# The opening of a hybrid decoder layer: memory rows turned before they are normed, and the memory keys and values projected for two row tiles per weight tile

## The chip, the cores and the metric

The kernel runs on one core of a Trainium2 chip. The metric is the device time of one execution in microseconds (us); three runs of the kernel before gave 2234.21, 2238.23 and 2239.06 us, and the median, 2238.23 us, is what the change is held against. Everything is computed in float32; matmuls run as three passes over operands that are split into a high and a low part.

## The reference

One layer, a sequence of 1024 tokens of width 1024, and 256 memory tokens. What the change touches is the norm of x and the preparation of the memory keys and values:

```python
h = rms_norm(x, norm_mix_g[l])
proj = h @ w_in[l]
...
def memory_cross_attention(q, mem, mem_g, w_kv, q_g, k_g):
    qh = rms_norm(q.reshape(bsz, seq, C_HEADS, C_DQK), q_g)
    mkv = rms_norm(mem, mem_g) @ w_kv
    mk, mv = jnp.split(mkv, [C_Q_W], axis=-1)          # 512 key columns, 1024 value columns
    mk = rms_norm(mk.reshape(bsz, -1, C_HEADS, C_DQK), k_g)
    ...
```

`rms_norm` multiplies each row by one number (the inverse root mean square of the row) and each column by a gain. Everything after (three branches, gates, output projection, MLP) is the same in both kernels.

## The kernel before, in words

`phase_x` is the opening, roughly the first 66 us of the program. It produces `hT` (the normed x, turned so that features lie on partitions, as a high and a low part for each of 8 feature blocks k), `mkT` (the turned memory keys) and `mv` (the memory values). The rest of the program needs all three; `branch_c`, which follows at once, starts with 24 matmuls for each of 8 token tiles on `hT`.

- **Memory.** Two tiles `mx` of 128 memory rows are loaded. `norm_rows` squares and sums a row on ScalarE (ACT, L231), turns the sum into 1/rms on GpSimd (POOL, L127 and L128) and multiplies the tile in place on VectorE (DVE, L233). Then TensorE (PE) transposes the tiles (L243, bank `tp`), and `split` writes the result as high part (ACT, L114) and low part (DVE, L115) into `memT`, with the gain.
- **Weights.** `load_w` brings `in_wkv` in pieces of 512 KB (`raw`, L137), and splits each into a high part (ACT, L111) and a low part (DVE, L112) in a tile `w`, which holds two of the eight blocks k. There are three buffers for `raw` and four for `w`.
- **Projections.** Group 0 of `wkv` gives the keys, groups 1 and 2 the values. For each group `proj` runs one row tile after the other: 8 blocks times three matmuls (`mm3`, L91) into one PSUM bank `mm`. A finished key tile is copied (L266), squared (L268), reduced per head (L270), turned into 1/rms (L127, L128), scaled (L273), transposed (L276) and split into `mkT`.
- **x.** Eight tiles `xk` are loaded (L293), normed the same way (L231, L127, L128, L233), transposed (L94, bank pair `sc`) and split into `hT`.

All DMAs are issued by one queue, SyncE's (SP), in order. Each engine executes its own queue in order. In `phase_x` the order of each queue is made by the framework's scheduler, which moves instructions of different steps past each other on PE as well; from `branch_c` on PE's order is pinned to the program's.

Of the kernel before, what the change touches and what calls it, by code (L numbers as in the profile page):

```python
# [10 lines left out]
F32 = mybir.dt.float32  # L11
F32R = mybir.dt.float32r
AF = mybir.ActivationFunctionType
ALU = mybir.AluOpType
AX = mybir.AxisListType
PSUM = bass.MemoryType.PSUM

P = 128
D = 1024
S = 1024  # L20
NT = 8
NK = 8
# [5 lines left out]
R_MIX, R_MEM, R_MLP, R_MN, R_CB, R_CW, R_BG = 0, 8, 16, 24, 32, 40, 72  # L28
# [43 lines left out]
class Layer:  # L72
# [152 lines left out]
        self.nlam = d[:, 37:38]  # L225


    def norm_rows(self, src, r1, scr):

        nc = self.nc  # L230
        nc.scalar.activation(scr, src, AF.Square, accum_out=r1)  # L231
        self.rsqrt_mean(r1, r1, D, 1)
        nc.vector.tensor_scalar_mul(src, src, r1)  # L233


    def mem_kv(self, pool, tmp, xs):
        nc, a = self.nc, self.a
        memT = tmp.tile([P, NK, 2, 256], F32R, tag="memT", name="memT")
        for k in range(0, NK, 2):
            ps = self.tp_tile()  # L240
            for i in range(2):
                for t in range(2):
                    nc.tensor.transpose(  # L243
                        ps[:, (i * 2 + t) * P : (i * 2 + t + 1) * P], xs[t][:, (k + i) * P : (k + i + 1) * P], self.ident
                    )
            for i in range(2):
                self.split(
                    memT[:, k + i, 0], memT[:, k + i, 1], ps[:, i * 256 : (i + 1) * 256],
                    self.vec[:, R_MEM + k + i : R_MEM + k + i + 1],
                )  # L250
        self.mkT = pool.tile([P, 4, 2, 256], F32R, name="mkT")
        self.mv = pool.tile([P, 2, 2, D], F32R, name="mv")

        def proj(w, t):
            ps = self.mm_tile()
            for k in range(NK):
                self.mm3(
                    ps, (memT[:, k, 0, t * P : (t + 1) * P], memT[:, k, 1, t * P : (t + 1) * P]), w[k], k == 0, k == NK - 1
                )
            return ps  # L260

        w = self.load_w(a["wkv"][0], 512, 2)
        for t in range(2):
            ps = proj(w, t)
            kr = tmp.tile([P, 512], F32, tag="kr", name=self.name("kr"))
            nc.scalar.copy(kr, ps)  # L266
            scr = tmp.tile([P, D], F32, tag="sq", name=self.name("scr"))
            nc.scalar.activation(scr[:, 0:512], ps, AF.Square)  # L268
            r4 = tmp.tile([P, 4], F32, tag="r4", name=self.name("r4"))
            nc.vector.tensor_reduce(r4, scr[:, 0:512].rearrange("p (h d) -> p h d", h=4), axis=AX.X, op=ALU.add)  # L270
            self.rsqrt_mean(r4, r4, 128, 4)
            for h in range(4):
                nc.vector.tensor_scalar_mul(kr[:, h * P : (h + 1) * P], kr[:, h * P : (h + 1) * P], r4[:, h : h + 1])  # L273
            pt = self.tp_tile()
            for h in range(4):
                nc.tensor.transpose(pt[:, h * P : (h + 1) * P], kr[:, h * P : (h + 1) * P], self.ident)  # L276
            p4 = pt.rearrange("p (h t) -> p h t", h=4)
            self.split(self.mkT[:, :, 0, t * P : (t + 1) * P], self.mkT[:, :, 1, t * P : (t + 1) * P], p4)
        for g in range(2):
            w = self.load_w(a["wkv"][1 + g], 512, 2)  # L280
            yield
            for t in range(2):
                ps = proj(w, t)
                s = slice(g * 512, (g + 1) * 512)
                self.split(self.mv[:, t, 0, s], self.mv[:, t, 1, s], ps)

    def phase_x(self, kv, tmp):

        nc, a = self.nc, self.a

        def load(src, tag):
            x = tmp.tile([P, D], F32, tag=tag, name=self.name(tag))
            nc.sync.dma_start(x, src)  # L293
            return x

        def norm(x):
            r = tmp.tile([P, 1], F32, tag="r1", name=self.name("r1"))
            scr = tmp.tile([P, D], F32, tag="sq", name=self.name("scr"))
            self.norm_rows(x, r, scr)

        mem = [load(a["mem"][t * P : (t + 1) * P, :], "mx") for t in range(2)]
        for x in mem:
            norm(x)
        gen = self.mem_kv(kv, tmp, mem)
        next(gen)
        xs = [load(a["x"][t * P : (t + 1) * P, :], "xk") for t in range(NT)]

        def half(hf):
            for x in xs[4 * hf : 4 * hf + 4]:
                norm(x)  # L310
            for k in range(NK):
                if k % 2 == 0:
                    sc = self.sc_tile()
                ps = sc[:, k % 2 * 512 : k % 2 * 512 + 512]
                for i in range(4):
                    self.transpose(ps[:, i * P : (i + 1) * P], xs[4 * hf + i][:, k * P : (k + 1) * P])
                s = slice(hf * 512, (hf + 1) * 512)
                self.split(self.hT[:, k, 0, s], self.hT[:, k, 1, s], ps, self.vec[:, R_MIX + k : R_MIX + k + 1])

        half(0)  # L320
        next(gen)
        half(1)
        for _ in gen:
            pass

    def store_y(self, b, kt, hf, y):
        self.nc.sync.dma_start(self.yd[b][kt, :, hf * 512 : (hf + 1) * 512], y)
# [1426 lines left out]
```

## Time and profile before

The profiled execution has a span of 2237.1 us from its first instruction to its last, 1.1 us under the median of the runs.

| what | measured |
|---|---|
| PE busy over the span | 2180.2 us (97%) |
| DVE, ACT, POOL busy | 1394.6, 1012.0, 534.1 us |
| first transposes of memory (PE) | 12.35 us |
| first projection matmul (PE) | 14.68 us |
| last transposes of x on PE | 65.30 us |
| first transposes of `branch_c` (tile `cqr`) | 70.78 us |

Almost the whole span is PE work in a fixed order, so what the opening takes longer or shorter moves all that follows. A timeline row reads: start, duration, engine, line, operation, out<-in, count, and in brackets how long the engine sat idle before it and what ended that.

### The profile page before, as it was taken

The page shows a single profiled execution, that of the slowest core. Times are in us where ns is not written, and L with a number is a line of the kernel's source. Part 1 is how long each engine was busy: PE and PEld are TensorE (multiplying, and loading weights), DVE is VectorE, ACT ScalarE, POOL GpSimd, SP SyncE. Part 2 cuts the span into 40 slices and gives each one's busy share as a digit, 9 for nine tenths or more (in the row PEclk, how much of TensorE's full clock was granted, in tenths as well). Part 3 has the DMA queues.
Part 4 walks back from the last instruction along what each step waited for, and adds up shares of the span by engine and source line. Part 5 has one row for each costly group of instructions (what it writes and reads, how often), then busy time and mean ns, then how long its engine had stood idle before and what let it go on. Part 6 is the DMA issues. An engine that isn't in the chain of part 4 may idle for free.

```text
span 2237.1 us, 30556 instructions
## 1 busy us (share of the span) xinstructions
PE 2180.2 (97%) x11222; PEld 1875.4 (84%) x11222; DVE 1394.6 (62%) x2627; ACT 1012.0 (45%) x1994; POOL 534.1 (24%) x696
## 2 busy tenths in 40 slices
PE   7999999999999999999999999999999999899999
PEld 5778788988799999999888888887887888788887
DVE  6645456554238888888752233453588887866679
ACT  6533445443336666666643111223444444543332
POOL 2100000000001111111000002202566666565553
PEclk9999999999999999999999999999999999999999
DMA  6013222210421001110134343435525444864444
GB/s 247 20 72 114 70 65 80 67 44 29 144 69 31 26 29 39 39 36 29 54 122 141 114 139 129 151 107 182 182 99 193 155 151 155 296 202 147 147 151 168
DMA packets 113780, 247.89 MB, mean 111 GB/s; under 512 B 11065, under 2 KB 19550, under 8 KB 111582
## 3 DMA queue, kind: packets, MB, share of 16 engines
q1 hardware_dynamic: 111326, 233.36, 31.6%
q10 hardware_dynamic: 2304, 12.58, 1.4%
q8 instruction: 88, 1.44, 0.3%
q14 instruction: 62, 0.51, 0.1%
HBM read 178.76 MB, written 67.14 MB: 110 GB/s over the span
## 4 chain that ended last, share of the span: by engine, by line
PE 78%; DVE 8%; DMA 5%; ACT 4%; issue 2%; POOL 1%; SPq 0%; DVEq 0%; ACTq 0%; POOLq 0%
PE mm L91 46%; PE p L91 21%; PE sc L91 6%; PE tp L94 2%; PE po L91 2%; PE pr L94 1%; DVE w L112 1%; DVE acc L67 1%; DMA raw<-in_wd 1%; DVE u L67 1%; DVE wo L67 1%; DMA kraw<-y 1%; ACT dpe L997 1%; ACT w L111 0%; DVE c L67 0%
## 5 line engine op out<-in xcount | busy, mean ns | idle before, releaser
L91 PE MATMUL mm<-w,hT 128*128 128x384 f32 (+3 forms) x2496 | 480.7, 332 | 2.6 <-ACT w L111 1.7
L91 PE MATMUL mm<-hT,w 128*128 128x512 f32 x1920 | 464.7, 396 | 2.8 <-ACT w L111 2.6
L91 PEld LDWEIGHTS mm<-hT,w 128*128 128x128 f32 x1920 | 355.2, 189 | 76.2 <-ACT w L111 2.8
L91 PEld LDWEIGHTS mm<-w,hT 128*128 128x128 f32 x2496 | 385.8, 189 | 14.9 <-ACT w L111 2.4
L91 PE MATMUL p<-xd,wo 128*128 128x512 f32 x1344 | 309.4, 392 | 5.6 <-DVE c L67 2.2
L91 PE MATMUL p<-xo,wo 128*128 128x512 f32 x1344 | 308.2, 390 | 5.5 <-DVE st L1407 1.8
L91 PEld LDWEIGHTS p<-xd,wo 128*128 128x128 f32 x1344 | 253.4, 189 | 61.5 <-DVE c L67 3.3
L91 PEld LDWEIGHTS p<-xo,wo 128*128 128x128 f32 x1344 | 251.0, 188 | 61.3 <-DVE u L67 3.7
L91 PE MATMUL mm<-kt,w 128*128 128x512 f32 x1152 | 261.6, 389 | 0.2 <-DVE w L112 0.2
L112 DVE TENSOR_TENSOR w<-raw,w 128x256 fp32r<-128x256 f32 (+3 forms) x304 | 171.9, 589 | 141.0 <-ACT w L111 139.7
L91 PEld LDWEIGHTS mm<-kt,w 128*128 128x128 f32 x1152 | 216.1, 188 | 45.5 <-DVE w L112 0.7
L111 ACT CAST w<-raw 128x256 fp32r<-128x256 f32 (+3 forms) x304 | 154.7, 531 | 177.4 <-PE mm L91 131.6
L104 ACT CAST wo<-wraw 128x896 fp32r<-128x896 f32 x122 | 115.0, 944 | 207.6 <-PE p L91 111.5
L67 DVE TENSOR_TENSOR wo<-wraw,wo 128x896 fp32r<-128x896 f32 x122 | 145.3, 1208 | 58.2 <-ACT wo L104 58.1
L1134 POOL TENSOR_TENSOR wraw<-wraw 128x128 f32<-128x128 f32 x128 | 96.8, 757 | 239.6 <-DMA wraw<-in_wdown 118.5
L997 ACT ACTIVATE dpe<-sc,dst,drr 128x256 f32<-128x256 f32 (+7 forms) x128 | 106.7, 834 | 52.3 <-DVE dst L993 49.0
L989 DVE CUSTOM_DVE_ANT_0 sc<-sc,tmask 128x256 f32<-128x256 f32 (+7 forms) x128 | 97.1, 759 | 22.0 <-PE sc L91 22.0
L127 POOL TENSOR_SCALAR hss<-hss 128x4 f32<-128x4 f32 x8 | 3.3, 412 | 392.5 <-ACT mscr L747 272.7
L127 POOL TENSOR_SCALAR drr<-drr 128x16 f32<-128x16 f32 x16 | 3.6, 225 | 373.6 <-DVE drr L943 357.0
L1137 POOL TENSOR_TENSOR wraw<-wraw 128x128 f32<-128x128 f32 x128 | 88.5, 692 | 10.0
L1136 POOL TENSOR_TENSOR wraw<-wraw 128x128 f32<-128x128 f32 x128 | 90.7, 709 | 0.0
L104 ACT CAST xd<-xd 128x1536 fp32r<-128x1536 f32 (+2 forms) x36 | 54.9, 1528 | 69.8 <-DMA xd<-r_d 69.7
(281 smaller groups left out, 3101.0 us busy)
## 6 DMA issues: line engine op xcount, KB each, us to landing
wraw<-in_wup SPq DMA_DIRECT2D x64, 256.0 KB, 3.2
r_d<-xts SPq DMA_DIRECT2D x16, 1024.0 KB, 4.1
wraw<-in_wdown SPq DMA_DIRECT2D x64, 256.0 KB, 3.1
xd<-r_d SPq DMA_DIRECT2D x19, 768.0 KB, 7.5
xd<-r_d SPq DMA_DIRECT2D x14, 1024.0 KB, 6.6
raw<-in_wgate SPq DMA_DIRECT2D x48, 256.0 KB, 3.1
gates<-gt SPq DMA_DIRECT2D x48, 256.0 KB, 2.0
raw<-in_wd SPq DMA_DIRECT2D x32, 384.0 KB, 3.6
```

The lines of the kernel that those rows point to most:

```text
L67: return self.tc.keep_in_program_order(f(*a, **k))
L91: self.pin(self.nc.tensor.matmul(out, l, r, start=start, stop=stop))
L94: self.pin(self.nc.tensor.transpose(out, x, self.ident))
L104: self.A.copy(hi, src)
L111: nc.scalar.copy(hi, src)
L112: nc.vector.tensor_sub(lo, src, f32(hi))
L127: g.tensor_scalar(r, ss, 1.0 / width, EPS, op0=ALU.mult, op1=ALU.add)
L989: V.tensor_tensor_reduce(out=sc[:, 0:n], in0=sc[:, 0:n], in1=self.tmask[:, D - n : D], scale=1.0, scalar=-3.0e38, op0=ALU.add, op1=ALU.max ...
L997: nc.scalar.activation(pe[c][:, 0:n], sc[:, 0:n], AF.Exp, bias=t8[:, 2 + c : 3 + c], scale=rr[:, i, c : c + 1], accum_out=t8[:, 4 + c : 5 ...
L1134: G.tensor_add(r[:, 4], r[:, 0], r[:, 3])
L1136: G.tensor_sub(r[:, 6], r[:, 1], r[:, 0])
L1137: G.tensor_sub(r[:, 7], r[:, 2], r[:, 5])
```

## The change

Memory rows are transposed raw. Their 1/rms (`rm`) is applied later, as the scale of the instructions that read the projections out of PSUM: for keys the copy and the square on ACT, for values the two halves of `split`. Each weight block now serves both row tiles before the next one (6 matmuls in place of 3), with two accumulation banks open. PE's order is pinned to the program's in the whole of `phase_x`. x's tiles are normed inside the first two passes, every second one by POOL in place of DVE; the transposes of x's first half stand in the second pass (in the `tp` banks), those of its second half in the third. The numbers of matmuls (144) and transposes (88) stay the same.

```diff
+    def row_scale(self, src, r1, scr):
+        self.nc.scalar.activation(scr, src, AF.Square, accum_out=r1)
         self.rsqrt_mean(r1, r1, D, 1)
-        nc.vector.tensor_scalar_mul(src, src, r1)
...
+        self.pinned = True
+        mem = [load(a["mem"][t * P : (t + 1) * P, :], "mx") for t in range(2)]
+        rm = [scale(x, f"rm{t}") for t, x in enumerate(mem)]
...
+        def proj(w, ps, k):
+            for t in range(2):
+                c = slice(t * P, (t + 1) * P)
+                self.mm3(ps[t], (memT[:, k, 0, c], memT[:, k, 1, c]), w[k], k == 0, k == NK - 1)
+
+        def keys(t, ps):
+            kr = tmp.tile([P, 512], F32, tag=f"kr{t}", name=self.name("kr"))
+            nc.scalar.activation(kr, ps, AF.Copy, scale=rm[t])
             scr = tmp.tile([P, D], F32, tag="sq", name=self.name("scr"))
+            nc.scalar.activation(scr[:, 0:512], ps, AF.Square, scale=rm[t])
...
+        def norm(t):
+            r = scale(xs[t])
+            (nc.gpsimd if t % 2 else nc.vector).tensor_scalar_mul(xs[t], xs[t], r)
+
+        w = self.load_w(a["wkv"][0], 512, 2)
+        mem_turn(0)
+        mem_turn(2)
+        xs.extend(load(a["x"][t * P : (t + 1) * P, :], "xk") for t in range(NT))
+        ps = [self.mm_tile() for _ in range(2)]
+        for k in range(NK):
+            proj(w, ps, k)
+            if k in (1, 3):
+                mem_turn(k + 3)
+            if k >= 4:
+                norm(k - 4)
+        kr = [keys(t, ps[t]) for t in range(2)]
+        w = self.load_w(a["wkv"][1], 512, 2)
+        sv = self.sc_tile()
+        pv = [sv[:, 0:512], sv[:, 512:]]
+        for k in range(NK):
+            proj(w, pv, k)
+            if k < 4:
+                norm(4 + k)
+            else:
+                x_turn(0, 2 * k - 8)
+                x_turn(0, 2 * k - 7)
+        values(0, pv)
+        w = self.load_w(a["wkv"][2], 512, 2)
+        ps = [self.mm_tile() for _ in range(2)]
+        for k in range(NK):
+            if k in (1, 3):
+                key_turn(k // 2, kr[k // 2])
+            proj(w, ps, k)
+            x_turn(1, k)
+        values(1, ps)
+        self.pinned = False
```

One stretch shows how the queues read now: the passage from the key pass to the first value pass, on ACT and on DVE. PE has nothing between the last key matmul and the first matmul on the values' first weight piece in the change; before, the second key tile's matmuls followed the first key tile's. In these rows the first number of a name is its running number: `xk_18` to `xk_25` are x's eight tiles in the change; `raw_8`, `raw_10`, `raw_12`, `raw_14` and `w_9` to `w_15` belong to the key pass; `w_45` to `w_51` to the first value pass; `kr_38` and `kr_41` are the two key tiles.

ACT in the change, from the square of the fourth x tile to the second weight piece of the first value pass:

```order
L230 ACTIVATE scr_37_294,r1_36_293<-xk_21_197 128x1024
L274 ACTIVATE kr_38_299<-mm_26_207,r1_4_140 128x512
L276 ACTIVATE scr_39_301<-mm_26_207,r1_4_140 128x512
L274 ACTIVATE kr_41_311<-mm_27_208,r1_6_145 128x512
L276 ACTIVATE scr_42_313<-mm_27_208,r1_6_145 128x512
L230 ACTIVATE scr_54_351,r1_53_350<-xk_22_199 128x1024
L230 ACTIVATE scr_56_363,r1_55_362<-xk_23_201 128x1024
L230 ACTIVATE scr_58_375,r1_57_374<-xk_24_203 128x1024
L111 CAST w_45_325<-raw_44_323 128x1024
L230 ACTIVATE scr_60_387,r1_59_386<-xk_25_205 128x1024
L111 CAST w_47_330<-raw_46_328 128x1024
```

And in the kernel before, from the last weight piece of the keys (`w_19`) on:

```order
L111 CAST w_19_208<-raw_18_206 128x1024
L114 ACTIVATE memT_152<-tp_11_180,vec_76 128x256
L111 CAST w_31_301<-raw_30_299 128x1024
L266 COPY kr_21_236<-mm_20_211 128x512
L268 ACTIVATE scr_22_238<-mm_20_211 128x512
L111 CAST w_33_306<-raw_32_304 128x1024
L111 CAST w_35_311<-raw_34_309 128x1024
```

The first weight piece of the values (`w_31` before, `w_45` now) stood ahead of the first key tile's copy; now it stands behind both key tiles' copies and squares and three squares of x.

DVE in the kernel before, over the same stretch:

```order
L112 TENSOR_TENSOR w_19_208<-raw_18_206,w_19_208 128x1024
L115 SCALAR_TENSOR_TENSOR memT_152<-tp_11_180,vec_76,memT_152 128x256
L112 TENSOR_TENSOR w_31_301<-raw_30_299,w_31_301 128x1024
L270 TENSOR_REDUCE r4_23_240<-scr_22_238 128x4
L273 TENSOR_SCALAR kr_21_236<-kr_21_236,r4_23_240 128x128 x4
L112 TENSOR_TENSOR w_33_306<-raw_32_304,w_33_306 128x1024
```

There the low part of the values' first weight piece (`w_31`) came ahead of the first key tile's norm. DVE in the change, from the first key tile's norm on (`r4_40` and `r4_43` are the key tiles' statistics, `r1_53` and `r1_57` those of `xk_22` and `xk_24`):

```order
L278 TENSOR_REDUCE r4_40_303<-scr_39_301 128x4
L281 TENSOR_SCALAR kr_38_299<-kr_38_299,r4_40_303 128x128 x4
L278 TENSOR_REDUCE r4_43_315<-scr_42_313 128x4
L312 TENSOR_SCALAR xk_22_199<-xk_22_199,r1_53_350 128x1024
L281 TENSOR_SCALAR kr_41_311<-kr_41_311,r4_43_315 128x128 x4
L312 TENSOR_SCALAR xk_24_203<-xk_24_203,r1_57_374 128x1024
L112 TENSOR_TENSOR w_45_325<-raw_44_323,w_45_325 128x1024
L112 TENSOR_TENSOR w_47_330<-raw_46_328,w_47_330 128x1024
```

The low part of `w_45` now stands behind the norms of both key tiles and the scaling of `xk_22` and `xk_24`. The statistics `r1` of x have two buffers, so the square of `xk_24` (which writes `r1_57`) waits until `xk_22` has been scaled with `r1_53`.

More of the change, by code (lines that the diff above doesn't have):

```diff
@@ L225, in consts @@
         self.nlam = d[:, 37:38]
-    def norm_rows(self, src, r1, scr):
-        nc = self.nc
-        nc.scalar.activation(scr, src, AF.Square, accum_out=r1)
+    def row_scale(self, src, r1, scr):
+        self.nc.scalar.activation(scr, src, AF.Square, accum_out=r1)
         self.rsqrt_mean(r1, r1, D, 1)
[L233 to L285, printed above, removed]
@@ L294, in load, with scale @@
             return x
-        def norm(x):
-            r = tmp.tile([P, 1], F32, tag="r1", name=self.name("r1"))
+        def scale(x, tag="r1"):
+            r = tmp.tile([P, 1], F32, tag=tag, name=self.name("r1"))
             scr = tmp.tile([P, D], F32, tag="sq", name=self.name("scr"))
-            self.norm_rows(x, r, scr)
+            self.row_scale(x, r, scr)
+            return r
+        self.pinned = True
         mem = [load(a["mem"][t * P : (t + 1) * P, :], "mx") for t in range(2)]
-        for x in mem:
-            norm(x)
@@ L304, in phase_x @@
[L304 to L311, printed above, removed]
-                if k % 2 == 0:
[L313 to L324, printed above, removed]
+        rm = [scale(x, f"rm{t}") for t, x in enumerate(mem)]
+        memT = tmp.tile([P, NK, 2, 256], F32R, tag="memT", name="memT")
+        self.mkT = kv.tile([P, 4, 2, 256], F32R, name="mkT")
+        self.mv = kv.tile([P, 2, 2, D], F32R, name="mv")
+        def mem_turn(k):
+            ps = self.tp_tile()
+            for t in range(2):
+                for i in range(2):
+                    j = i * 2 + t
+                    self.transpose(ps[:, j * P : (j + 1) * P], mem[t][:, (k + i) * P : (k + i + 1) * P])
+            for i in range(2):
+                self.split(
+                    memT[:, k + i, 0], memT[:, k + i, 1], ps[:, i * 256 : (i + 1) * 256],
+                    self.vec[:, R_MEM + k + i : R_MEM + k + i + 1],
+                )
@@ new lines, in proj @@
+        def proj(w, ps, k):
+            for t in range(2):
+                c = slice(t * P, (t + 1) * P)
[3 more added lines that the diff above has]
+            nc.scalar.activation(kr, ps, AF.Copy, scale=rm[t])
+            scr = tmp.tile([P, D], F32, tag="sq", name=self.name("scr"))
+            nc.scalar.activation(scr[:, 0:512], ps, AF.Square, scale=rm[t])
+            r4 = tmp.tile([P, 4], F32, tag="r4", name=self.name("r4"))
+            nc.vector.tensor_reduce(r4, scr[:, 0:512].rearrange("p (h d) -> p h d", h=4), axis=AX.X, op=ALU.add)
+            self.rsqrt_mean(r4, r4, 128, 4)
+            for h in range(4):
+                nc.vector.tensor_scalar_mul(kr[:, h * P : (h + 1) * P], kr[:, h * P : (h + 1) * P], r4[:, h : h + 1])
+            return kr
@@ new lines, in key_turn, with values @@
+        def key_turn(t, kr):
+            pt = self.tp_tile()
+            for h in range(4):
+                self.transpose(pt[:, h * P : (h + 1) * P], kr[:, h * P : (h + 1) * P])
+            p4 = pt.rearrange("p (h t) -> p h t", h=4)
+            self.split(self.mkT[:, :, 0, t * P : (t + 1) * P], self.mkT[:, :, 1, t * P : (t + 1) * P], p4)
+        def values(g, ps):
+            s = slice(g * 512, (g + 1) * 512)
+            for t in range(2):
+                self.split(self.mv[:, t, 0, s], self.mv[:, t, 1, s], ps[t], rm[t])
@@ new lines, in phase_x, with x_turn @@
+        xs, sc = [], {}
+        def x_turn(hf, k):
+            if hf == 0:
+                ps = self.tp_tile()
+            else:
+                if k % 2 == 0:
+                    sc[hf] = self.sc_tile()
+                ps = sc[hf][:, k % 2 * 512 : k % 2 * 512 + 512]
+            for i in range(4):
+                self.transpose(ps[:, i * P : (i + 1) * P], xs[4 * hf + i][:, k * P : (k + 1) * P])
+            s = slice(hf * 512, (hf + 1) * 512)
+            self.split(self.hT[:, k, 0, s], self.hT[:, k, 1, s], ps, self.vec[:, R_MIX + k : R_MIX + k + 1])
@@ new lines, in phase_x @@
+        kr = [keys(t, ps[t]) for t in range(2)]
[6 more added lines that the diff above has]
+                norm(4 + k)
+            else:
+                x_turn(0, 2 * k - 8)
[8 more added lines that the diff above has]
+            x_turn(1, k)
```

## The prediction

> **What bounds the kernel now.** I read the page first, then the opening by windows, PE's timeline and the chain of waits there, and last the groups of instructions of the first 71 us, which price the queues.
>
> ```profile
> span 2237.1 us, 30556 instructions
> ```
>
> The windows of the opening follow; columns are the stretch, its length, busy us and count for PE, its weight loads, DVE, ACT and POOL, then granted clock, DMA share and GB/s.
>
> ```profile
> 0.00:12.30 12.30, 0.45 (x1) 0.18 (x1) 1.91 (x11) 5.17 (x8) 2.89 (x13) 1.00 0.77 285
> 12.30:21.00 8.70, 8.48 (x34) 6.64 (x35) 7.24 (x16) 4.28 (x8) 0.03 (x1) 1.00 0.52 170
> 21.00:30.00 9.00, 7.82 (x36) 6.07 (x36) 5.50 (x10) 6.01 (x9) 1.21 (x2) 1.00 0.68 231
> 30.00:41.00 11.00, 9.29 (x43) 6.69 (x43) 7.93 (x14) 8.45 (x15) 6.14 (x10) 1.00 1.00 405
> 41.00:66.00 25.00, 24.88 (x138) 20.18 (x138) 24.00 (x31) 21.77 (x35) 4.46 (x8) 1.00 0.37 115
> ```
>
> After 12.3 us PE is nearly full, but DVE and ACT are full as well from 41 us on. So PE's idle time here is small, and it is a matter of three engines' queues, not of PE's work. PE's timeline gives the start, the chain gives the end of the opening and PE's pace.
>
> ```profile
> 12.35 0.69 PE L243 MATMUL tp<-ident,mx 128*128 128x128 f32 x2 [4.79 <-DVE mx L233]
> 14.68 3.81 PE L91 MATMUL mm<-w,memT 128*128 128x512 f32 x10
> 25.20 0.59 ACT L266 COPY kr<-mm 128x512 f32<-128x512 f32 x1 [1.46 <-PE mm L91]
> 65.90 5.04 PE mm L91 x22
> 70.95 0.44 PE tp L94 x4
> ```
>
> A matmul costs 5.04 / 22 = 0.229 us and a transpose 0.44 / 4 = 0.11 us. The first ten matmuls take 3.81 us, 0.38 each: PE begins slowly. The mark that I compare is the first transposes of `branch_c`, at 70.95 us; before them stand 144 + 36 matmuls (41.2 us) and 88 transposes (9.7 us), so from 12.35 us on PE loses 70.95 - 12.35 - 50.9 = 7.7 us. That is nearly all a better order could win, besides an earlier start.
>
> **The change part by part.** The prices of the queue steps are the mean durations, the second number behind the first bar, in ns:
>
> ```profile
> L112 DVE TENSOR_TENSOR w<-raw,w 128x1024 fp32r<-128x1024 f32 x16 | 19.4, 1217 | 0.5 <-ACT w L111 0.4
> L111 ACT CAST w<-raw 128x1024 fp32r<-128x1024 f32 x16 | 16.6, 1052 | 2.0 <-DMA raw<-in_wkv 1.0 <-DMA raw<-in_wcq 0.6 <-PE mm L91 0.3
> L115 DVE SCALAR_TENSOR_TENSOR hT<-sc,vec,hT 128x512 fp32r<-128x512 f32 x16 | 11.2, 744 | 0.2
> L114 ACT ACTIVATE hT<-sc,vec 128x512 fp32r<-128x512 f32 x16 | 10.3, 697 | 2.4 <-PE sc L94 2.4
> L231 ACT ACTIVATE scr<-xk 128x1024 f32<-128x1024 f32 x8 | 8.6, 1070 | 0.3 <-DVE xk L233 0.3
> L128 POOL TENSOR_TENSOR r<-r,mhalf 128x1 f32<-128x1 f32 x10 | 6.3, 634 | 0.7
> L233 DVE TENSOR_SCALAR xk<-xk,r 128x1024 f32<-128x1024 f32 x8 | 6.0, 751 | 2.7 <-POOL r L128 2.4
> L127 POOL TENSOR_SCALAR r<-r 128x1 f32<-128x1 f32 x10 | 3.8, 380 | 20.0 <-ACT scr L231 19.8
> L115 DVE SCALAR_TENSOR_TENSOR memT<-tp,vec,memT 128x256 fp32r<-128x256 f32 x8 | 3.8, 480 | 2.0 <-ACT memT L114 2.0
> L128 POOL TENSOR_TENSOR r<-r,mhalf 128x4 f32<-128x4 f32 x2 | 2.0, 1016 | 0.2
> L273 DVE TENSOR_SCALAR kr<-kr,r 128x128 f32<-128x128 f32 x8 | 1.7, 280 | 2.6 <-POOL r L128 2.6
> L270 DVE TENSOR_REDUCE r<-scr 128x4 f32<-128x512 f32 x2 | 1.4, 684 | 1.1 <-ACT scr L268 1.1
> L268 ACT ACTIVATE scr<-mm 128x512 f32<-128x512 f32 x2 | 1.2, 612 | 0.0
> ```
>
> PE's work is unchanged: the same 144 matmuls and 88 transposes. So every term is a wait.
>
> *The start.* The raw transposes no longer wait for the norm.
>
> ```profile
> 8.21 1.06 ACT L231 ACTIVATE scr<-mx 128x1024 f32<-128x1024 f32 x1 [3.00 <-DMA mx<-in_mem]
> 9.43 1.06 ACT L231 ACTIVATE scr<-mx 128x1024 f32<-128x1024 f32 x1
> 10.68 1.04 ACT L111 CAST w<-raw 128x1024 fp32r<-128x1024 f32 x1
> ```
>
> They can run at 8.3 and 9.5 us instead of 12.35. But ACT still squares both memory tiles first and then casts the first weight piece (to 11.7), and only then reads the transposes. The high half of `memT` comes at 12.1, the low half of w at 11.7 + 1.22 = 12.95, that of `memT` at 13.4. Products begin at 12.1 and flow from 13.4, about 2 us earlier than 14.68: the saving on the way in is 2 us, not 4. Spacing of the squares is 9.43 - 8.21 = 1.22 us, which I use for all of them.
>
> *The key pass.* Two blocks of memory now stand on DVE behind a scaling of x: block 3 behind `xk_18`, block 7 behind `xk_20`. For `xk_18`: third cast done at 14.8, square to 16.0, POOL 0.38 + 0.63 to 17.1, scaling 0.75, low half 0.48: 18.3 us. For `xk_20` the same steps, behind the square of `xk_19` and its POOL scaling, end at 25.3. PE needs 24 matmuls for each tile, 11.0 us, 8 more transposes 0.9 us, and loses about 2 us to the slow beginning; block 7's products end at 26.3 us for the first row tile and 27.0 for the second. Before, the first key tile alone was done at 25.2. So far nothing is lost: both tiles are done where one was, and one pass of 24 matmuls (5.5 us) is in hand less 1.8.
>
> *The gap behind it.* This is the term that decides. The values' first weight piece (`w_45`) stands on ACT behind both key tiles' reads and three squares, and the third of those (`xk_24`) writes a statistic whose buffer is free only after `xk_22` was scaled, which DVE does behind the first key tile's norm. From 26.3 us: read 0.59 and square, 27.4; reduce 0.68, 28.2; POOL 0.2 + 1.02 with its issue, 29.5; four scalings, 30.4; second reduce, 31.0; scaling of `xk_22` 0.75, 31.8; square of `xk_24`, 33.1; cast 1.05, 34.2. The low half comes later still, since DVE scales `xk_24` first: POOL, from 29.5 on, does the statistics of `xk_22` (1.0), of the second key tile (1.2, held up by DVE to 33), of `xk_23` (1.0), the scaling of `xk_23` itself, and those of `xk_24` (0.9). With 1.2 us for that scaling POOL is done at 36.2, `xk_24` is scaled at 37.0, and `w_45` is whole at 38.2 us. PE stands from 27.0 to 38.2 but for one matmul: 11 us, where the row 21.00:30.00 shows 1.2 us idle before.
>
> POOL's scaling of 1024 columns does not occur in this trace. The nearest rows are a fill of the same size and a two-input operation on half of it:
>
> ```profile
> L1670 POOL MEMSET tmask<- 128x1024 f32 x1 | 1.0, 956 | 19.1 <-ACT w L111 19.1
> L1336 POOL TENSOR_TENSOR mg<-mg,gl 128x512 f32<-128x512 f32 x16 | 20.5, 1288 | 155.4 <-DVE gl L1334 155.4
> ```
>
> So between 0.96 and 2 x 1.29 = 2.6 us; one input is nearer to the fill, and I take 1.2. It stands once on this chain, and weakly a second time in front of block 7, so the ends are -0.3 and +2 us.
>
> *The slow restart.* A stop of PE shows a price of its own later in this trace:
>
> ```profile
> 112.77 2.79 PE L91 MATMUL sc<-cpT,mv 128*128 128x512 f32 x6 [1.97 <-ACT cpe L380]
> 109.50:112.90 3.40, 1.44 (x7) 0.86 (x6) 1.53 (x5) 3.40 (x11) 1.20 (x2) 1.00 0.00 0
> 112.90:116.40 3.50, 3.50 (x11) 2.82 (x12) 1.87 (x6) 0.30 (x1) 0.00 (x0) 0.51 0.20 75
> ```
>
> After 3.4 us in which PE was busy for 1.44, the next 3.5 us ran at 0.51 of the clock, a loss of 1.7 us. Eleven idle us must trigger this too. I take 2.5 us: the 1.7 of that row plus half of it, as products may restart in the middle of such a stretch; the ends are 0 and, for two such stretches, 3.4.
> [...]
>
> *The value passes.* From 38.2 us: the first takes 47 matmuls 10.8, 32 transposes 3.5, the restart 2.5, and 1.2 of waits, since each pair of transposes needs its two banks read (0.70 on ACT, 0.74 on DVE) behind casts: 56.2 us. The second takes 48 matmuls 11.0, 40 transposes 4.4 and 0.7 of waits, 72.3. With 36 matmuls of `branch_c` (8.2) the mark falls at 80.5 us.
>
> *DMA and the rest.* The squares wait for x, whose loads are now issued behind the fourth weight piece in one run.
>
> ```profile
> xk<-in_x SPq DMA_DIRECT2D x8, 512.0 KB, 8.7
> raw<-in_wcq SPq DMA_DIRECT2D x4, 512.0 KB, 4.3
> ```
>
> Issued from 13 us on and landing 1.3 us apart, `xk_24` is there near 26 us, before its square at 31.8; `raw_44`, near 28, before its cast. `raw_50` is issued when `w_45` is split, lands 4.3 us later at 42.5 and is needed near 46. All that is hidden under the gap; without the gap the x loads would be late by 1 to 2 us. The 1/rms at the evictions costs nothing that shows (one operand on instructions that exist). `branch_c` and what follows hang on PE alone, so the shift stays.
>
> The sum: 80.5 - 70.95 = 9.6 us later. The profiled execution's span, 2237.1, lies 1.1 under the median; the forecast for the median is 2238.2 + 9.6 = 2247.8 us. A measurement here tells about 0.2% (4.5 us) from no change.
>
> **The rivals.** *A, same:* the gap is shorter. If the key pass ends 1.5 us earlier (a quick clock at the start), POOL takes 0.96, there is no slow restart and the value passes lose nothing (1.9), then 9.6 - 1.5 - 0.3 - 2.5 - 1.9 = 3.4, or 2241.6 us. For it: each number here is a mean. Against: the chain's nine steps are fixed by the queues.
>
> *B, faster:* PE does not stop, because the first value weights are ready when the key pass ends. Gap 11.2 and restart 2.5 fall away: 9.6 - 13.7 = -4.1, and with dense value passes -6.0, so 2232.2 us. It decides where PE's stop between the passes is under 1 us. For it: `raw_44` lands near 28 us. Against: the cast stands where the queue puts it.
>
> *C, slower still:* POOL and DVE shut each other out. The trace has it:
>
> ```profile
> 32.89 1.23 DVE L112 TENSOR_TENSOR w<-raw,w 128x1024 fp32r<-128x1024 f32 x1
> 32.91 1.26 POOL L127 TENSOR_SCALAR r<-r 128x4 f32<-128x4 f32 x1 [4.51 <-DVE r L270]
> ```
>
> A statistic that takes 0.2 us elsewhere ended with DVE's split. If scalings take 2.6 us and DVE stands behind them, the chain grows by 1.4 to 2 us and the key pass by 1, the restart by 0.9: 9.6 + 4 = 13.6, or 2251.8 us. [...]
>
> **How the numbers follow.** The forecast's case has 0.66, C 0.12, A 0.16, B 0.06. The range 2240 to 2253 us takes in A's price, C's and the unknown ends, and leaves out B and the edges. Slower by over 0.2% is the forecast and C, 0.78; within 0.2% is A, 0.16; faster is B, 0.06.
>
> **What would show it.** Right: PE idle for 9 to 12 us between the last key matmul and the second matmul on `w_45`, put down first to ACT's cast and then to DVE's split; the square of `xk_24` waiting on DVE's scaling of `xk_22`; the granted clock near half for 3 to 7 us behind it; first transposes on PE at 8 to 9.5 us; the mark near 80 us. Wrong: a stop under 5 us there, the mark before 75 us, or a time under 2242.7 us.

## The result, and the profile after

| | before | changed |
|---|---|---|
| median of four runs, us | 2238.28 (2234.21 to 2239.06) | 2252.95 (2249.61 to 2256.85) |
| span of the profiled execution, us | 2237.1 | 2249.1 (time 2250.91) |
| the mark (first transposes of `branch_c`), us | 70.78 | 86.46 |

The ratio is 1.0071, 95% interval 1.0056 to 1.0087: slower by 12.5 to 19.5 us on 2238. The forecast was 2247.8; the side was right, the size was 5 us too small. The mark comes 15.7 us later, where 9.6 were forecast. Matching products on PE stay 15.2 to 17.2 us late up to about 900 us, and 15 us late up to 1550 us. By the end of these two executions 12.0 us are left: 1.5 us go at about 1560 us, where before has 6.8 us of half clock and the changed kernel 3.4, and another 1.5 us go in small steps up to 1950 us, whose cause stays open. I use the mark below: it lies ahead of that scatter.

PE's timeline of the changed kernel (start, length, instructions; in brackets the idle time before, and what ended it):

```profile
8.54 0.69 PE L94 MATMUL tp<-ident,mx 128*128 128x128 f32 x2 [0.68 <-DMA mx<-in_mem]
12.49 5.46 PE L91 MATMUL mm<-w,memT 128*128 128x512 f32 x12 [1.14 <-ACT memT L114]
27.27 1.20 PE L91 MATMUL mm<-w,memT 128*128 128x512 f32 x4 [0.97 <-DVE memT L115]
36.19 0.79 PE L91 MATMUL sc<-w,memT 128*128 128x512 f32 x1 [7.72 <-ACT w L111]
42.14 9.65 PE L91 MATMUL sc<-w,memT 128*128 128x512 f32 x29 [5.16 <-DVE w L112]
60.47 1.65 PE L91 MATMUL mm<-w,memT 128*128 128x512 f32 x6
78.16 8.46 PE L91 MATMUL mm<-w,hT 128*128 128x512 f32 x36
86.46 0.60 PE L94 MATMUL tp<-ident,cqr 128*128 128x128 f32 x4
```

The stop is there, with both forecast releasers: first ACT's cast of `w_45`, then DVE's split. It lasts from 28.5 to 42.1 us, 13.6 us with one product in it. The timelines of ACT, POOL and DVE show why it is longer than 11 us. ACT's, with the square of `xk_24` and the cast of `w_45`:

```profile
34.05 1.06 ACT L230 ACTIVATE scr<-xk 128x1024 f32<-128x1024 f32 x1 [1.56 <-DVE xk L312]
...
35.11 1.03 ACT L111 CAST w<-raw 128x1024 fp32r<-128x1024 f32 x1
```

The square waits for DVE's scaling of `xk_22`, as forecast, and the cast comes at 35.1 (33.1 forecast). POOL's four scalings:

```profile
22.26 2.86 POOL L312 TENSOR_SCALAR xk<-xk,r 128x1024 f32<-128x1024 f32 x1
27.61 2.85 POOL L312 TENSOR_SCALAR xk<-xk,r 128x1024 f32<-128x1024 f32 x1
36.40 2.85 POOL L312 TENSOR_SCALAR xk<-xk,r 128x1024 f32<-128x1024 f32 x1
42.60 4.40 POOL L312 TENSOR_SCALAR xk<-xk,r 128x1024 f32<-128x1024 f32 x1
```

And DVE's waits for POOL:

```profile
26.07 0.75 DVE L312 TENSOR_SCALAR xk<-xk,r 128x1024 f32<-128x1024 f32 x1 [3.41 <-POOL r L128]
31.89 0.87 DVE L281 TENSOR_SCALAR kr<-kr,r 128x128 f32<-128x128 f32 x4 [2.10 <-POOL r L128]
40.20 0.75 DVE L312 TENSOR_SCALAR xk<-xk,r 128x1024 f32<-128x1024 f32 x1 [4.12 <-POOL r L128]
40.87 3.49 DVE L112 TENSOR_TENSOR w<-raw,w 128x1024 fp32r<-128x1024 f32 x3
```

A scaling on POOL takes 2.85 us, not 1.2. Three of them stand in the chain, each in front of a statistic that DVE waits for: the one at 22.26 before block 7 of the memory, the one at 27.61 before the first key norm, the one at 36.40 before the scaling of `xk_24`, behind which `w_45` is split. Next, windows: two of the 15 us from the key pass on (before, then changed), and the half-clock stretch with the time after the restart.

```profile
27.00:42.00 15.00, 12.12 (x58) 8.53 (x57) 10.51 (x20) 10.29 (x18) 7.82 (x14) 1.00 0.89 346
```

```profile
27.00:42.00 15.00, 1.99 (x5) 0.96 (x5) 5.70 (x14) 9.41 (x15) 13.13 (x15) 0.63 0.26 102
30.90:47.95 17.05, 6.60 (x15) 4.84 (x16) 8.04 (x15) 7.67 (x12) 14.39 (x13) 0.50 0.26 83
42.14:47.95 5.81, 5.81 (x14) 4.55 (x15) 3.10 (x3) 1.21 (x2) 4.75 (x2) 0.50 0.77 243
42.14:51.63 9.49, 9.49 (x30) 7.47 (x30) 4.79 (x5) 3.31 (x4) 4.75 (x2) 0.69 0.71 225
```

In 27 to 42 us DVE was busy 5.7 us where it was 10.5 before, and POOL, not PE, was the full engine. The clock was granted at half for 17.05 us and came back 5.81 us after the products did.

### The profile page after: what moved, and what is told of

Same layout as the page of the kernel before. It is cut to its first block, busy times and chain, and to the rows that moved or that the text cites. A ratio compares the mean times of both kernels' runs of the same rounds, so it can differ in the third digit from the quotient of the medians.

```text
span 2249.1 us, 30540 instructions
## 1 busy us (share of the span) xinstructions
PE 2186.1 (97%) x11222; PEld 1879.7 (84%) x11222; DVE 1389.9 (62%) x2621; ACT 1013.6 (45%) x1994; POOL 539.7 (24%) x700
## 4 chain that ended last, share of the span: by engine, by line
PE 80%; DVE 8%; DMA 5%; ACT 4%; POOL 2%; issue 2%; SPq 0%; DVEq 0%; ACTq 0%; POOLq 0%
PE mm L91 46%; PE p L91 22%; PE sc L91 6%; PE tp L94 2%; PE po L91 2%; PE pr L94 1%; DVE w L112 1%; ACT w L111 1%; DVE acc L67 1%; DMA raw<-in_wd 1%; DVE wo L67 1%; DVE u L67 0%; ACT dpe L1018 0%; DMA wraw<-in_wup 0%; DMA x_d<-gl 0%
```

## The experiments

All marks and ratios stand side by side here; each ratio is to the kernel before on the same chip. A mark is read from one execution, and executions differ by chance from the first products on: the last transposes of memory, ahead of which the queues are alike, come at 20.62 us in run 8 and at 21.73 us in run 2. So a difference of marks under about 1 us shows nothing by itself. By their ratios runs 1, 2, 3, 7 and 8 cannot be told from the changed kernel, since their intervals overlap its own; for these the argument rests on the marks and on the rows.

| run | mark, us | ratio (95%) |
|---|---|---|
| changed kernel | 86.46 | 1.0071 (1.0056 to 1.0087) |
| 1 x scaled on DVE | 82.24 | 1.0042 (1.0025 to 1.0059) |
| 2 filling products | 85.85 | 1.0070 (1.0053 to 1.0087) |
| 3 value weights first | 84.28 | 1.0055 (1.0040 to 1.0071) |
| 4 raw turn alone, on before | 69.96 | 0.9989 (0.9977 to 1.0001) |
| 5 other queues | 79.43 | 1.0031 (1.0018 to 1.0043) |
| 6 the same with POOL | 81.01 | 1.0031 (1.0021 to 1.0041) |
| 7 filling, 7 buffers | 83.91 | 1.0060 (1.0043 to 1.0076) |
| 8 7 buffers | 86.04 | 1.0059 (1.0041 to 1.0076) |
| 9 other queues, turns spread | 75.50 | 1.0020 (1.0010 to 1.0031) |
| 10 other queues, PE's order free | 72.37 | 1.0004 (0.9990 to 1.0019) |
| 11 as 9, 7 buffers | 78.00 | 1.0029 (1.0018 to 1.0040) |
| 12 changed, PE's order free | 82.14 | 1.0026 (1.0009 to 1.0042) |

**1. POOL's scalings.**

```diff
-            (nc.gpsimd if t % 2 else nc.vector).tensor_scalar_mul(xs[t], xs[t], r)
+            nc.vector.tensor_scalar_mul(xs[t], xs[t], r)
```

> All eight x tiles are scaled on DVE, as before the change; POOL keeps only the statistics. The mark is the first branch_c transposes on PE: 70.8 us before, 86.5 after. Theory (the stop of PE behind the key pass is set by the queues, and POOL's 2.85-us scalings stand in that chain): block 7 of the memory is no longer late by POOL, the key pass ends about 1.4 us earlier, the norm of the first key tile no longer waits 2.1 us for POOL, w_45 is whole near 38 instead of 42.1, the mark comes at 81 to 83, the time falls by 4 to 5 us. Rival (DVE is the fullest engine here, POOL's help is what the change needs): DVE gets 4 x 0.75 = 3 us more work, the mark comes at 87 to 89. Rival (late weights): no change, mark within 1 us of 86.5.

PE's timeline:

```profile
34.91 0.80 PE L91 MATMUL sc<-w,memT 128*128 128x512 f32 x1 [7.03 <-ACT w L111]
38.45 8.99 PE L91 MATMUL sc<-w,memT 128*128 128x512 f32 x29 [2.74 <-DVE w L112]
82.24 0.60 PE L94 MATMUL tp<-ident,cqr 128*128 128x128 f32 x4
```

`w_45` is whole at 38.45 instead of 42.14, and the mark comes 4.2 us earlier, although DVE has 3 us more to do. POOL's scalings cost 4 of the 15.7 us. (38.45 is also within 0.3 us of the 38.2 that the prediction reached with a cheap scaling, but partly by luck: the key pass ends at 27.9 here, where 27.0 was forecast, and the gap behind it lasts 10.6 us, where 11.2 was.)

**2. The slow restart.**

```diff
         pv = [sv[:, 0:512], sv[:, 512:]]
+        fill = memT[:, 0].rearrange("p a t -> p (a t)")
+        for i in range(55):
+            self.mm(pv[0], memT[:, 0, 0, 0:P], fill, start=True, stop=True)
```

> 55 products of memT with itself are put on PE ahead of the first value pass, into the bank that this pass then overwrites: they keep PE busy for 12.6 us from the end of the key pass, so to 41.1, just short of the 42.1 at which the first value weights are whole. Nothing of the computation changes. Theory (PE's slow restart costs 2.5 to 2.9 us of its own): the granted clock stays at 1.0, the value weights are whole at 42.1 as in the changed kernel, the 29 products behind it take 6.7 us instead of 9.5, the mark comes at 83 to 84. Rival (the products behind the stop were slow because they waited for weights and for transposes, the clock was not the limit): the mark stays at 86 to 87. Rival (the added products get in the way): mark later than 87.

The window of the 29 products behind the stop:

```profile
42.88:49.74 6.86, 6.86 (x29) 5.48 (x30) 3.43 (x3) 1.21 (x2) 4.75 (x2) 1.00 0.70 226
```

PE's timeline, the first wait for `hT` and the mark:

```profile
54.02 1.31 PE L94 MATMUL tp<-ident,xk 128*128 128x128 f32 x8 [1.85 <-DVE hT L115]
85.85 0.60 PE L94 MATMUL tp<-ident,cqr 128*128 128x128 f32 x4
```

ACT's and DVE's timelines ahead of that wait:

```profile
49.75 1.06 ACT L111 CAST w<-raw 128x1024 fp32r<-128x1024 f32 x1 [2.08 <-DMA raw<-in_wkv]
50.84 2.46 DVE L112 TENSOR_TENSOR w<-raw,w 128x1024 fp32r<-128x1024 f32 x2 [1.91 <-ACT w L111]
```

The clock stayed at 1.00 and the products took 6.86 us instead of 9.49, 2.6 less, as expected. But the mark moved by 0.6 only, where the theory had 2.5 to 3.5. Counted from the moment `w_45` is whole, which came 0.74 later here because of the later start, it moved by 1.35. PE then waits 1.85 us for a low half of `hT`: it stands on DVE behind splits of weights that had only just landed, since their loads wait for a raw buffer that the split of `w_45` frees. The restart's price was real, and about half of it or more was hidden. Runs 7 and 8 test that.

**3. The value weights ahead in the queues.**

```diff
+        keep = self.tc.keep_in_program_order
...
+                keep(nc.scalar.copy(t[:, 0], raw))                # pieces 1 and 2 of wkv[1]
+                keep(nc.vector.tensor_sub(t[:, 1], raw, f32(t[:, 0])))
...
+            self.kept(nc.scalar.activation(scr, xs[t], AF.Square, accum_out=r))   # x tiles 4 to 7
```

> ACT casts and DVE splits the four weight pieces of the first value pass ahead of the squares and scalings of x tiles 4 to 7 (the third to sixth step behind the key reads); everything else is as in the changed kernel, with POOL's scalings. Theory (the place of w_45 in ACT's and DVE's queues makes the stop): cast of w_45 at 30.5 to 31.5, its low half behind both key norms near 35, so 7 us earlier than 42.1; a stop of 6 to 7 us is left and with it the slow clock; mark at 79 to 81. Rival (the weights land late, or the buffer is late): w_45 whole at 40 or later, mark within 1 us of 86.5. Rival (the pass over both row tiles, or PE's written order, is at fault whatever the queues do): stop shorter, but the time comes back in the value passes, which then wait for the x tiles 4 to 7; mark at 85 or later.

PE's timeline:

```profile
31.53 0.63 PE L91 MATMUL sc<-w,memT 128*128 128x512 f32 x1 [2.75 <-ACT w L341]
37.15 9.22 PE L91 MATMUL sc<-w,memT 128*128 128x512 f32 x29 [4.99 <-DVE w L342]
50.96 1.31 PE L94 MATMUL tp<-ident,xk 128*128 128x128 f32 x8 [2.33 <-DVE hT L115]
84.28 0.60 PE L94 MATMUL tp<-ident,cqr 128*128 128x128 f32 x4
```

ACT's, at the fourth value piece:

```profile
40.93 1.05 ACT L111 CAST w<-raw 128x1024 fp32r<-128x1024 f32 x1 [7.56 <-DMA raw<-in_wkv]
```

The stop is 5 us shorter (37.15), but the mark gains only 2.2: my theory missed, and the second rival (the time comes back in the value passes) is nearer. ACT stands 7.56 us for the fourth piece's load with the squares of x queued behind it, and the low halves of `hT` are late again. Taking the weights forward alone moves the wait into the value pass.

**4. The raw turn alone.**

```diff
-        for x in mem:
-            norm(x)
...
+            nc.scalar.activation(scr, mem[t], AF.Square, accum_out=rm[t])
+            self.rsqrt_mean(rm[t], rm[t], D, 1)
...
-            nc.scalar.copy(kr, ps)
+            nc.scalar.activation(kr, ps, AF.Copy, scale=rm[t])
...
-                self.split(self.mv[:, t, 0, s], self.mv[:, t, 1, s], ps)
+                self.split(self.mv[:, t, 0, s], self.mv[:, t, 1, s], ps, rm[t])
```

> The kernel before with one part of the change alone: memory turned without its norm, 1/rms applied where the products are read. One row tile after the other, x scaled on DVE, PE's order left to the scheduler. Theory (this part is a small gain): first transposes at 8.5 instead of 12.3 us, products from about 13, the mark 1 to 2 us earlier than 70.8, so 69 to 70. Rival (DVE and ACT are full in 41 to 66 us, so an earlier start is given back there): mark at 70.5 to 71. Rival (the raw turn or the scaling at the evictions is itself dear): mark later than 72.

```profile
12.22 4.67 PE L91 MATMUL mm<-w,memT 128*128 128x512 f32 x9 [0.93 <-ACT memT L114]
69.96 0.60 PE L94 MATMUL tp<-ident,cqr 128*128 128x128 f32 x4
```

Products begin 2.5 us earlier (PE's timeline), the mark comes 0.8 earlier. The rest is given back ahead of the stretch in which DVE and ACT are full (from 41 us on): the first transposes of x come at 36.53 us where they came at 37.23, 0.7 earlier. ACT's reads of a key tile take 0.69 and 0.68 us with the scale (27.81 and 28.39 us in the changed kernel), where they took 0.59 and 0.60 (25.20 and 25.69 us before), and no loss from that shows at the mark. So this part shows no cost. It is the only version here below the kernel before, and its interval reaches 1.0001, so that it beats before is not shown.

**5 and 6. All queues in another order.** Loads, casts and splits stand as the expectation says; PE's order is that of the changed kernel.

```diff
+        xs.extend(load(a["x"][t * P : (t + 1) * P, :], "xk") for t in range(4))
+        for k0 in (0, 2, 4):
+            fetch(k0)                    # loads of the value weights, pieces 1 to 3
+        xs.extend(load(a["x"][t * P : (t + 1) * P, :], "xk") for t in range(4, NT))
+        fetch(6)
...
+            if k in (5, 7):              # in the key pass
+                piece()                  # cast and split, kept in this order on ACT and DVE
```

> The changed kernel with the same products and transposes in the same order on PE, but other queues: SP loads x tiles 0 to 3, then three value weight pieces, then x tiles 4 to 7; ACT and DVE cast and split the first two value pieces inside the key pass, the third and fourth ahead of the key norms and of the squares of x tiles 4 to 7; all x tiles are scaled on DVE. Theory (the queues make the whole loss, the pass over both row tiles and the raw turn cost nothing): w_45 whole at 26 to 28, before the key pass ends; no stop over 2 us, no half clock; the value passes go at DVE's pace, some 34 us for both, so the mark comes at 69 to 72 (before: 70.8, changed: 86.5). Rival (one weight pass for both row tiles needs each weight piece twice as fast, so PE starves whatever the queues do): stops of 1 to 2 us at each piece, mark at 75 to 79. Rival (the loads: value weights and x compete): w_45 whole after 30, mark at 74 or later.

> As the run with the other queues, but the odd x tiles are scaled on POOL (2.85 us each) as in the changed kernel. Theory (POOL's scalings only hurt where somebody waits for POOL behind them): they stand in front of the statistics of the next x tile and of the key norm, and DVE and POOL hold each other up; DVE has 3 us less to do, but waits more: mark 0 to 3 us later than with DVE's scalings. Rival (POOL's help pays once nothing waits): mark 1 to 3 us earlier.

Run 5, what PE waited for between 12 and 90 us (total, times, longest):

```profile
PE tp L94 <- DVE hT L115: 3.5, 2, 2.3
PE sc L91 <- DVE w L330: 2.5, 3, 1.1
PE sc L94 <- DVE hT L115: 2.5, 3, 2.2
```

The window of 42 to 57 us:

```profile
42.00:57.00 15.00, 9.54 (x47) 7.39 (x47) 13.77 (x18) 12.15 (x18) 3.67 (x5) 0.89 0.38 113
```

DVE's timeline at the first x transposes, and PE's at the mark:

```profile
37.59 1.41 DVE L115 SCALAR_TENSOR_TENSOR hT<-tp,vec,hT 128x512 fp32r<-128x512 f32 x2 [2.88 <-ACT hT L114]
79.43 0.60 PE L94 MATMUL tp<-ident,cqr 128*128 128x128 f32 x4
```

`w_45` is whole at 28.1, and the 12.9 us that PE waited for the first value piece (7.72 + 5.16) have become 2.5 on three pieces. The mark still comes at 79.43, where I expected 69 to 72: the queues are not the whole loss. PE now waits 6 us for low halves of `hT`, at 0.89 of the clock, while DVE, full in 42 to 57 us (13.77 of 15), had stood 2.88 us at 37.6 because PE's order had brought no x transpose yet. Stops at each weight piece, the rival, are only 2.5 us. Run 6, with the odd tiles on POOL, reaches the mark 1.6 us later (the theory's side) and has the same ratio.

**7 and 8. The clock and the loads.** Seven raw buffers, with the filling products of run 2 and without.

```diff
-                    self.rp = E2(name="rp", bufs=3)
+                    self.rp = E2(name="rp", bufs=7)
```

> As the run with the 55 filling products, with 7 buffers for raw weights instead of 3, so that the fourth value piece and those of the second value pass land before w_45 is split. Theory (the clock's 2.6 us were hidden because behind the stop DVE's splits waited for these loads, which wait for a buffer that the split of w_45 frees): with both taken away the fourth piece is there at once, the first low half of hT comes 2 us earlier after w_45, the mark comes at 83.5 to 84.5. Rival (the weight tile's own ring of 4, or DVE's work, is what counts): mark at 85.5 to 86.

> The changed kernel with 7 buffers for raw weights instead of 3, no filling products. Theory (behind the stop the slow clock and the late loads lie beside each other, and either alone hides the other): w_45 whole at 42 as before, 29 products in 9.5 us, the mark within 0.7 us of 86.5. Rival (the late loads alone cost what the slow clock was taken to cost): mark at 84 to 85.

PE's timelines, run 7 and run 8:

```profile
42.19 7.03 PE L91 MATMUL sc<-w,memT 128*128 128x512 f32 x29 [0.97 <-DVE w L112]
83.91 0.60 PE L94 MATMUL tp<-ident,cqr 128*128 128x128 f32 x4
```

```profile
41.89 9.45 PE L91 MATMUL sc<-w,memT 128*128 128x512 f32 x29 [5.16 <-DVE w L112]
86.04 0.60 PE L94 MATMUL tp<-ident,cqr 128*128 128x128 f32 x4
```

Both marks are as expected. The buffers alone move the mark by 0.4 us, the warm clock alone by 0.6, both by 2.5. Counted from the moment `w_45` is whole, which leaves out the chance of the start, it is 0.2, 1.35 and 2.6 us. Either way the two together gain more than their sum: slow clock and late loads lie partly beside each other.

**9, 10 and 12. PE's written order.** Run 9 spreads the transposes in run 5's kernel; runs 10 and 12 leave PE's order to the scheduler, in run 5's and in the changed kernel.

```diff
-            if k < 4:
-                norm(4 + k)
-            else:
-                x_turn(0, 2 * k - 8)
-                x_turn(0, 2 * k - 7)
+            x_turn(0, k)
+            if k >= 4:
+                norm(k)
```

```diff
-        self.pinned = True
+        self.pinned = False
```

> The kernel with the other queues, and one more edit: in the first value pass the eight groups of x transposes stand one behind each weight step, where the changed kernel writes two behind each of the last four steps. PE's written order is the only difference, the work is the same. Theory (the written order holds the transposes back until the pass is half over, DVE stands 2.9 us for them, and then all its work comes at once, so PE waits 5.7 us on low halves of hT and the clock halves twice): waits on hT in the first value pass under 2 us, at most one half-clock stretch, mark at 72 to 76 instead of 79.4. Rival (DVE has too much to do whatever PE's order is): mark at 78 to 80. Rival (one pass for both row tiles starves PE at each weight piece): stops before the first product of each piece, mark above 77.

> The kernel with the other queues, with PE's order left to the scheduler as before the change (it mixes transposes among products one or two at a time, and begins the second value pass's products and transposes while the first pass's are still under way). Theory (the written order is what is left of the loss): mark at 73 to 76. Rival (DVE's work, or the pass over both row tiles): mark at 78 to 80.

> The changed kernel with PE's order left to the scheduler, as before the change; loads, POOL's scalings and the place of the value weights' casts behind the squares are as in the changed kernel. With the other queues, PE's order was worth 7.1 us (79.4 to 72.4). Theory (the stop and the written order are two terms; the order frees little while w_45 comes late): w_45 whole at 41 to 43 as before, some of the x transposes move into the stop, which shortens the first value pass by 2 to 4 us; mark at 82.5 to 85. Rival (the written order alone was the loss): mark at 79 or earlier. Rival (it only helps once the queues are right): mark at 86 to 87.

The windows of 42 to 57 us, run 9 and then run 10:

```profile
42.00:57.00 15.00, 12.16 (x59) 9.07 (x57) 13.77 (x17) 10.94 (x18) 5.40 (x8) 0.89 0.44 132
```

```profile
42.00:57.00 15.00, 13.44 (x73) 9.77 (x72) 13.84 (x19) 12.43 (x19) 3.11 (x4) 1.00 0.39 120
```

The marks of runs 9 and 10 stand in the table. Of run 12, the products on the whole `w_45` and the mark:

```profile
42.36 9.71 PE L91 MATMUL sc<-w,memT 128*128 128x512 f32 x35 [0.66 <-DVE w L112]
82.14 0.60 PE L94 MATMUL tp<-ident,cqr 128*128 128x128 f32 x4
```

In 42 to 57 us DVE is equally full in runs 5, 9 and 10 (13.8 of 15), but PE does 47, 59 and 73 instructions. All three fall on the theory's side, runs 10 and 12 with marks slightly ahead of its ranges (73 to 76 and 82.5 to 85). In run 9 two edits lie together: the transposes spread, and with them the squares and scalings of x tiles 4 to 7 moved behind the fourth step; I did not try them apart. PE's free order takes the mark from 79.43 to 72.37, and on the changed queues from 86.46 to 82.14 with `w_45` as late as before. So there are two terms. They are not simply additive: freed order is worth 7.1 us on the good queues and 4.3 on the bad ones. Run 10 still turns raw and passes both row tiles together, and its ratio is 1.0004: in these queues the pass over both tiles costs no more than the 1.6 us by which its mark lies behind the kernel before, or 2.4 behind run 4, which has the raw turn alone.

**11. More raw buffers with the spread order** (run 9 with the edit of run 8).

> As the run with the transposes spread over the first value pass, with 7 buffers for raw weights instead of 3, so that the fourth value piece and the second pass's weights land earlier. Theory (with the stop gone, the loads' wait for a free buffer is what comes next): mark 1 to 3 us earlier than without the buffers, 70 to 74. Rival (DVE's work bounds it, or the weight tile's ring of 4): mark within 0.7 us of that run.

PE's timelines of run 9 and of run 11, the transposes of memory behind the first twelve products, and the stretch where the marks part:

```profile
17.16 0.60 PE L94 MATMUL tp<-ident,mx 128*128 128x128 f32 x4
50.80 2.91 PE L91 MATMUL mm<-w,memT 128*128 128x512 f32 x6
54.25 0.66 PE L94 MATMUL sc<-ident,xk 128*128 128x128 f32 x4 [0.54 <-DVE hT L115]
```

```profile
18.03 0.64 PE L94 MATMUL tp<-ident,mx 128*128 128x128 f32 x4
55.13 0.67 PE L94 MATMUL sc<-ident,xk 128*128 128x128 f32 x4 [2.11 <-DVE hT L115]
55.55 2.82 PE L91 MATMUL mm<-w,memT 128*128 128x512 f32 x6
```

This is a miss for every theory: the mark comes 2.5 us later than in run 9, not earlier. I put it down to chance, not to the buffers, but the rows show that for a part only. Of the 2.5 us, 0.9 are there from the first products on (17.16 and 18.03), and they are still 0.9 at 54.25 and 55.13. The other 1.6 come from the place of a half-clock stretch of 3.4 us. In run 9 it lies at 50.2 to 53.6 (0.89 of the clock in 42 to 57 us), on products behind which PE would have waited for DVE anyway: they take 2.91 us, and the wait is only 0.54. In run 11 it lies at 55.7 to 59.1 (0.95 in 42 to 57 us, 0.93 in 57 to 72), after that wait (2.11), and slows the products of the next step to 2.82 us. The two stretches begin 5.5 us apart; that this too is chance is an estimate of mine, and no run shows what sets their place. The ratios, 1.0020 and 1.0029, do not tell the two runs apart. More buffers did not help.

## Why the prediction was right and wrong

- **The bound: right.** The opening is a matter of three queues; PE's work did not change. The forecast named the stop, its place, its two releasers and the slow clock, and all are there.
- **The start: right.** The transposes come at 8.54 and 9.81, the first products at 12.49, and the second block of 12 at 18.1.
- **The key pass: 1.47 us short.** Its end was put at 27.0 for the second tile and is 28.47. Block 7 stands behind the statistic of `xk_20`, and that behind POOL's first scaling. The prediction had this as a weak second place. In run 1 the products from the last transposes of memory to the end of the pass take 1.2 us less (22.02 to 27.88, against 21.39 to 28.47 here); that is POOL's share.
- **The gap: the failed step.** "one input is nearer to the fill, and I take 1.2" was wrong: 2.85 us, above even the upper end of 2.6. And it stands on the chain three times, not "once on this chain, and weakly a second time". The stop grew from 11 to 13.6, and with the later key pass `w_45` was whole at 42.1 instead of 38.2, 3.9 of the 6.0 us that the mark missed. Run 1 shows it: with scalings at 0.75 us on DVE, `w_45` is whole at 38.45, 3.7 us earlier.
- **The slow restart: right in size, wrong in what it is worth.** 2.5 us were forecast, 1.7 from the row at 112.90 and the rest an estimate, and it costs PE 2.6. But taken away alone it moves the mark by 0.6 (1.35 from the whole `w_45` on); the sum added it in full to waits that it partly hides. The late loads, which the prediction put under the gap, are worth 0.2 us alone (run 8) and 1.25 once the clock is warm (run 7 against run 2, both from the whole `w_45` on).
- **The value passes: 0.3 and 1.6 us short.** 42.14 to 60.47 is 18.3 us (18.0 forecast); 60.47 to 78.16 is 17.7 (16.1). PE's waits for low halves of `hT` are not the main reason: in the first pass they are 0.6 us (1.2 forecast for all waits), in the second 1.2 in three waits (0.7 forecast). The products were priced too low: six of them between two groups of transposes take 1.48 us (60.47 to 61.95), where 0.229 us each gives 1.37. That the first pass comes out within 0.3 us is partly luck. With 1.47 + 2.47 + 0.33 + 1.59 and 0.10 at `branch_c` these are the 6.0 us by which the mark passes 80.5. (The sum set out from 70.95, a time in the chain of waits, where PE's timeline has 70.78 for the same transposes, 0.2 us less.)
- **Rival B rested on a wrong premise.** It said that without the stop the mark gains 13.7 us. Run 5 takes the stop away and gains 7.0: PE's written order was a second cause, hidden behind the first. Only with both taken away (run 10) does the mark gain 14.1. The prediction's 1.9 us for waits in dense value passes was a guess on that side as well.
- **Rival C was nearest in size** (2251.8), with its mechanism in part: scalings of 2.85 us with DVE behind them. Of POOL and DVE shutting each other out the rows show POOL's side alone, at 42.60: 4.40 us beside three splits, 1.55 more than without, while the splits take 1.22 us each, against 1.23 for the next one, at 47.07. That scaling is the last one, `xk_25`, and what it cost at the mark was not separated. Just ahead of it a statistic at 41.09 took 1.41 us, beside the same splits, where the others of its kind took 0.55 to 0.66.

## What to carry to other kernels

Price a step on an engine that has not done it yet by the worse of the nearest rows, and count every place where somebody waits for that engine's queue, the small statistic behind the big scaling above all. A price that is measured on an engine (a slow restart, a late load) is not a full gain until what lies beside it goes too. When a written order replaces a scheduler's, look at where it puts the groups that feed the fullest engine: here they stood bunched in the second half of a pass, and the scheduler's order was worth 7.1 us. Removing the first stop only shows the next. And before two marks are compared, see how far apart the executions were before the edit could act.

## What the runs showed of the hardware

POOL scales 128x1024 by a column in 2.85 us where DVE takes 0.75, 3.8 times as long, though its fill of that size takes 0.96. Beside DVE's splits it took 4.40: the scaling begins at 42.60, the splits end at 44.36, and it takes 1.55 us more than the others. The three splits took 1.22 us each there.

PE's first twelve products take 5.21 us in run 5, 5.46 in the changed kernel and 5.95 in run 1, 0.43 to 0.50 each, where later ones take 0.23 to 0.25. No half clock is recorded there: the windows of 12 to 27 us show 1.00 in all three, and the changed kernel's trace has no record of the clock ahead of 17.2 us. What slows these products no run shows. Between runs 9 and 11 the transposes behind them are 0.9 us apart (17.16 and 18.03).
